# Order of loads at a passage between two stages, one gate tile moved, and filler around 32x32 products in a hybrid encoder block

## The chip, the cores and the metric

The kernel runs on one core of a Trainium2 chip. The metric is the time of one execution in microseconds of device time (us); a kernel is timed in several runs, and their median counts. The engines are named as in the profile: PE (the matrix engine), PEld (its weight loads), DVE (vector), ACT (scalar), POOL (GpSimd) and SP, whose queue issues most of the DMA transfers.

## What is computed

One layer of a bidirectional encoder, 1024 tokens of width 1024, all in 32-bit floats. Cut to what matters here:

```
h   = rms_norm(x)
z   = h @ in_w                      # columns: attention q,k,v | RWKV | two sets of 1024 gates
att = windowed_gqa(q, k, v, sink)   # each token sees +-128 tokens, 8 query heads, 2 key heads
rwk = rwkv7 scans, forward and backward, summed, normed, gated   # 8 heads of 64
x   = x + (tanh-gates * (att @ w_up_attn) + tanh-gates * (rwk @ w_up_rwkv)) @ w_out
x   = x + squared_relu(rms_norm(x) @ w1) @ w2
x   = x + a gated per-layer embedding
```

A gate is written as 1 + tanh(z/2), up to a factor.

## The kernel before

**Products.** A float product on PE is made of three faster ones. Each operand is split into a rounded "hi" part, which ACT casts (`split`, L199), and the rest "lo", which DVE or POOL subtracts (L200). Then hi by hi, lo by hi and hi by lo are summed in one bank. The gates are tiles of 128 columns by 512 tokens: 8 such triples, 24 wide matmuls of 128x512 each (tile `gmm`). Weights of a gate tile come in two transfers (`wst`, halves a and b), which need a free one of the staging buffers; then ACT casts `whi`, the lo engine makes `wlo`, PE multiplies, ACT takes the tanh (`gth`, L333), and SP stores it to DRAM (`g_d`, L334).

**Stages.** First come the norm and the qkv products, then the RWKV operands of four head pairs, which are written to DRAM (`ra_d`, `bk_d`, `v_d`); the 16 gate tiles of the first half of the tokens, gates(0, m), are strewn into it. At its end the keys `kT` and the first queries `qT0`, `qT1` are read back (L756 to L771). Then comes attention in eight blocks n (L908 to L995): its last part at low priority is the rest of the first half's gates and, by `GATT`, the gate tile (1,0), the first of the second half. Into attention two things are mixed for the scans: low products (`lps`), and a triangular inverse by substitution on DVE (31 steps of a product, L837, and a sum, L840, then two transposes `Zn` and `Zt`, L847 and L848, and copies into `zi`, L869).

**The scans.** Sixteen chunks s of 64 tokens, forward and backward at once, in blocks of `NB` = 4. Chunk s multiplies the operands `rac` and `bkc` (`gps`, masked by DVE into `gm`, L1183), transposes (`tmps`, L1200), carries the state (`wy`), applies the inverse (`ups`), updates the state (`sps`) and adds outputs. Between these parts `gap(i)` takes `FILL[i]` steps from a filler, a generator named `beside` (L1000): 15 gate tiles of 24 steps, 6 empty steps (`BRIDGE`), and 16 tiles of 12 steps of the attention's up-projection (`uaps`), 558 steps in all. While a block runs, DVE works on the inverse for the next block, a few steps at a time (`TURNS`). Behind the last chunk of a block stands `end_inverse`: 128 products of 32x32 (`qps<-Zn,lt`), ACT copies them into `Q` (L866), `FILLQ` filler steps run between, then 128 more (`qps<-Zt,Q`), which ACT copies into `zi` (L879, L880). Next comes chunk s+1 with `wy`. A first `end_inverse(0, ...)` stands ahead of the loop, with the products of chunks 0 and 1 around it, and 4 filler steps (`FILL0`) behind each.

**What sets the order.** Products marked `mmo` and DVE steps marked `turn` stay in the program's order; other work is put in by a scheduler by priority and readiness. Each engine runs its list in order, so one instruction that waits holds all behind it; this goes for the DMA issues on the queues of SP and POOL too. The attention result comes back for the up-projection through `load_at` (issues at L1003, tiles named `gm` in the trace, four transfers from `at_d`) and its weights through `load_wu` (`wust`, issues at L1007).

Of the kernel before, what the change touches and what calls it, by code (L numbers as in the profile page):

```python
# [52 lines left out]

FILL0 = 4

GATT = 1
GQ = ((0, 1), (0, 2))

BRIDGE = 6
FILL = (5, 5, 3, 5, 3, 2, 4, 1)  # L60
FILLEND = 2

FILLEP = 11

LEAD = 1
FILLQ = 8
TURNS = ((0, 0, 4), (3, 2, 5), (3, 2, 5), (4, 3, 1))

LOW_AT = (3, 4)
# [77 lines left out]
def block_kernel(ctx: ExitStack, tc: tile.TileContext, I: dict, out: bass.AP):  # L147
# [39 lines left out]
    def after(ins, prev):  # L187

        tc.add_manual_dep(
            ins.ins, prev.ins.name,  # L190
            mybir.DependencyInfo(mybir.DependencyClass.NoSync, mybir.DependencyReason.DATA),
            reason="keep_in_program_order")
# [328 lines left out]
    with ExitStack() as s1:  # L521
# [127 lines left out]
        def fill0(p, i):  # L649

            if p == NP - 1:
                for _ in range(F0[i]):
                    next(gates0)
# [101 lines left out]

        kT = PY.tile([P, 2, 2, T], F32R, name="kT", tag="yk")  # L756
        qT0 = Q0.tile([P, NH, P], F32R, name="qT", tag="q0", bufs=1)
        nc.gpsimd.dma_start(qT0, qT_d[0])
        bands = Q0.tile([P, 3 * P + NH], F32, name="band", tag="q2", bufs=1)
        band = bands[:, 0:3 * P].rearrange("p (b t) -> p b t", b=3)  # L760
        nc.sync.dma_start(band, I["band"])
# [2 lines left out]
        for q in range(4):  # L764
            ts = slice(256 * q, 256 * q + 256)
            a = nc.gpsimd.dma_start(kT[:, :, :, ts], kT_d[:, :, :, ts])
            if q:
                after(a, on_pool[0])
            fill0(NP - 1, 1)
        qT1 = Q0.tile([P, NH, P], F32R, name="qT", tag="q1", bufs=1)  # L770
        nc.gpsimd.dma_start(qT1, qT_d[1])  # L771
        for _ in bonus:
            pass

# [2 lines left out]
    NB = 4  # L777
# [122 lines left out]
    def load_ra(s, d):  # L900
        return nc.sync.dma_start(ra_t[s % NRA, d], ra_d[d, chunk(s, d)])

    def load_bk(s, d):
        return nc.sync.dma_start(bk_t[s % NBK, d], bk_d[d, chunk(s, d)])

    lts, zzs, lows = {}, {}, {}
    with ExitStack() as s2:
# [16 lines left out]
        for n in range(NT):  # L924
            qT = queries(n) if n > 1 else (qT0, qT1)[n]
            k0, k1 = max(n - 1, 0), min(n + 2, NT)
            nk = k1 - k0
            b0 = k0 - (n - 1)
            pTs = []
            for kv in range(2):  # L930
                hs = slice(4 * kv, 4 * kv + 4)
                mx = A3.tile([P, 4], F32, name="mx", bufs=2)
                nm = A3.tile([P, 4], F32, name="nm", bufs=2)
                sums = A3.tile([P, 4], F32, name="sums", bufs=2)
                es = A3.tile([P, 4], F32, name="es", bufs=2)
                sm = A3.tile([P, 4, 3 * P], F32, name="smk", bufs=2)
                for h in range(4):
                    sc = PA.tile([P, nk * P], F32, name="sc", tag="sc", bufs=2)
                    for j in range(2):
                        nc.tensor.matmul(sc, qT[:, 4 * kv + h, :], kT[:, kv, j, k0 * P:k1 * P], start=(j == 0), stop=(j == 1))  # L940
                    nc.vector.tensor_tensor_reduce(
                        out=sm[:, h, 0:nk * P], in0=sc, in1=band[:, b0:b0 + nk, :].rearrange("p b t -> p (b t)"), scale=1.0,
                        scalar=-3.0e38, op0=ALU.add, op1=ALU.max, accum_out=mx[:, h:h + 1])
                nc.vector.scalar_tensor_tensor(out=nm, in0=mx, scalar=-0.125, in1=nsink[:, hs], op0=ALU.mult, op1=ALU.min)
                nc.vector.tensor_tensor(out=es, in0=sink[:, hs], in1=nm, op=ALU.add)
                nc.scalar.activation(out=es, in_=es, func=AF.Exp)
                for h in range(4):
                    nc.scalar.activation(out=sm[:, h, 0:nk * P], in_=sm[:, h, 0:nk * P], func=AF.Exp, scale=0.125, bias=nm[:, h:h + 1],
                                         accum_out=sums[:, h:h + 1])
                nc.vector.tensor_tensor(out=es, in0=es, in1=sums, op=ALU.add)  # L950
                nc.vector.reciprocal(es, es)
                pT = A3.tile([P, 3, 4, P], F32, name="pT", bufs=3)
                pTs.append(pT)
                for h in range(4):
                    if h % 2:
                        nc.scalar.activation(out=sm[:, h, 0:nk * P], in_=sm[:, h, 0:nk * P], func=AF.Copy, scale=es[:, h:h + 1])
                    else:
                        nc.vector.tensor_scalar_mul(sm[:, h, 0:nk * P], sm[:, h, 0:nk * P], es[:, h:h + 1])
                    pt = PA.tile([P, 3, P], F32, name="pt", tag="tp", bufs=3)
                    for j in range(nk):  # L960
                        nc.tensor.transpose(pt[:, j, :], sm[:, h, j * P:(j + 1) * P], ident)
                    if h % 2 == 0:
                        nc.vector.tensor_copy(pT[:, 0:nk, h, :], pt[:, 0:nk, :])
                    else:
                        nc.scalar.copy(pT[:, 0:nk, h, :], pt[:, 0:nk, :])
            po = PA.tile([P, 4, P], F32, name="po", tag="po", bufs=1)
            for j in range(nk):
                for kv in (1, 0):
                    nc.tensor.matmul(po[kv * 64:kv * 64 + 64], V[:, k0 + j, kv * 64:kv * 64 + 64], pTs[kv][:, j, :, :], start=(j == 0), stop=(j == nk - 1))
            at = A3.tile([P, 4, P], F32, name="at", bufs=1)  # L970
            nc.scalar.copy(at, po)
            put = nc.sync.dma_start(at_d[:, :, n * P:(n + 1) * P], at)
            if n == 0:
                low0 = low_products(BI, A2, 2, ps_att, 0, nc.tensor.matmul, put)
                next(low0)
            if n == 1:
                zi = zi_tile(BI, "zi")
            if n in LOW_AT:
                for _ in range(NB // len(LOW_AT)):
                    lts[0] = next(low0)  # L980
            if n == LOW_AT[-1]:
                for d in range(ND):
                    for a in (load_ra(0, d), load_bk(0, d)):
                        after(a, put)
            if n == INV_AT:
                zzs[0] = inverse_turned(BI, inverse(BI, lts[0]))
# [13 lines left out]
    def beside():  # L1000
# [4 lines left out]
        def load_wu(pl, m):  # L1005
            st = pl.tile([P, NP, P], F32, name="wust", tag="wu_st", bufs=2)
            nc.sync.dma_start(st, I["w_up_attn"][m])  # L1007
            return st

        load_at(0)  # L1010
        sts = [load_wu(B, m) for m in range(2)]
        yield from gates(1, range(GATT, 2 * KT), mmo, lo_of=lambda m: nc.vector)
        sW.close()
        sH1.close()
        epi["RWA"] = pool(sR, "rwA", side="right")
# [48 lines left out]
    def fill(n=1 << 30):  # L1064

        for _ in range(n):
            if next(filler, 0) == 0:
                break
# [270 lines left out]
    operand_tiles(B, (2, 3), (1, 2))  # L1339
    for s in (1, 2):  # L1340
        for d in range(ND):
            load_ra(s, d)
            load_bk(s, d)
    load_v(0)
    begin_low(1)
# [5 lines left out]
    was = []  # L1351

    def second_step():
        fill(FILLQ)
        wa = wa_tile()
        for h in range(NH):
            w_own(0, h, wa)
        was.append(w_copy(wa))
        for hf in range(2):
            products(1, hf)  # L1360
            fill(FILL0)
# [5 lines left out]
    for s in range(NCH):  # L1367
        more, nxt = s + 2 < NCH, s + 1 < NCH
        if s % NB == NB - 1 and s // NB < 2:
            begin_low(s // NB + 2)  # L1370

        def gap(i):

            fill(FILL[i] if more else FILLEND)

        def aside(i):

            b = s // NB + 1
            if b < NCH // NB and (s % NB, i) in ((0, 0), (0, 1), (0, 2), (0, 3)):
                low(b, i)  # L1380
            if ep is not None:
                next(ep, None)

        if s == 12:
            epi["E"] = BI
            ep = epilogue(0)
        carried(s)
        w_sum(s, W)
        if more:
            products(s + 2, 0)  # L1390
            load_next(s + 2)
        if nxt:
            load_v(s + 1)
        gap(0)
        aside(0)
        inverse_turn(TURNS[s % NB][0])
        gap(1)
        W = u_part(s, W)
        if more:
            products(s + 2, 1)  # L1400
        inverse_turn(TURNS[s % NB][1])
        gap(2)
        gap(3)
        aside(1)
        if nxt:
            s_part(s)
        y_part(s)
        aside(2)
        gap(4)
        if s % NB == 0 and s // NB < 3:  # L1410
            aside(3)
            inv[0] = inverse_steps(s // NB + 1)
        inverse_turn(TURNS[s % NB][2])
        gap(5)
        if nxt:
            operands(s + 1)
        gap(6)
        gap(7)
        if s % NB == NB - 1 and s // NB < 3:
            end_inverse(s // NB + 1, lambda: fill(FILLQ))  # L1420
        if s % NB or s // NB >= 3:
            aside(3)
    for _ in ep:
# [599 lines left out]
```

## Time and profile before

| what | value |
|---|---|
| three timed runs, us | 1676.85, 1670.13, 1672.34 |
| their median, us | 1672.34 |
| profiled execution, us | 1677.99 |
| its span, first to last instruction, us | 1676.2 |
| mean granted clock of PE | 0.984 |
| attention's end and the passage into the scans | about 455 to 500 us of the span |
| block ends in the scans (second products of 32x32) | 560, 628 and 704 us of the span |

A profile shows one execution. A row of its timeline has the start and the length in us, engine, line, operation, output<-inputs, the shape and the count; in square brackets stands how long the engine was idle before it and what it waited for. The windows give, for a stretch of time, the busy us of each engine and PEclk, the clock that was granted to PE as a share of the full one. "SPq" is the issue of a DMA on SP's queue; the transfer lands later.

### The profile page before, as it was taken

To read this page: it belongs to the slowest core of one execution; us is meant where nothing else is said; L and a number is where in the kernel's file an instruction comes from. 1 tells how busy PE (TensorE), PEld (TensorE's weight loads), DVE (VectorE), ACT (ScalarE), POOL (GpSimd) and SP (SyncE) were. 2 spreads that over 40 slices of the span, in tenths; PEclk is the share of its full clock that TensorE was granted. 3 is DMA by queue.
4 is the path that set the end of the run, shared out by engine and by line. 5 is a ranking of instruction groups with operands and counts; after the bars stand their busy time and mean duration, and the time that the engine had idled before them with its cause. 6 is when DMAs were issued, how large, how long until landed. Compare 5 with 4: busy or idle time off the path is not lost.

```text
span 1676.2 us, 31183 instructions
## 1 busy us (share of the span) xinstructions
PE 1609.2 (96%) x12280; PEld 1302.1 (78%) x12280; DVE 1156.5 (69%) x2103; ACT 820.7 (49%) x1485; POOL 104.8 (6%) x117
## 2 busy tenths in 40 slices
PE   7999999999879999899999999999999999999998
PEld 7987777666558787676778788888888888888887
DVE  6648998476938797876745886667667867675342
ACT  5548887378524443465314454444435445544121
POOL 3430000321200000000000000000000000000000
PEclk9999999999979999899999999999999999999999
DMA  6352555854377464547643154444459865564110
GB/s 224 83 150 88 174 171 182 252 161 145 103 212 199 141 183 129 171 147 231 207 170 113 51 191 146 159 153 143 145 173 351 276 192 172 160 211 145 39 41 38
DMA packets 200579, 269.24 MB, mean 161 GB/s; under 512 B 47728, under 2 KB 103920, under 8 KB 200432
## 3 DMA queue, kind: packets, MB, share of 16 engines
q1 hardware_dynamic: 190176, 253.09, 47.6%
q0 software_dynamic: 10112, 13.63, 3.0%
q8 instruction: 96, 1.57, 0.4%
q10 hardware_dynamic: 144, 0.52, 0.1%
q14 instruction: 51, 0.42, 0.1%
HBM read 186.45 MB, written 80.74 MB: 159 GB/s over the span
## 4 chain that ended last, share of the span: by engine, by line
PE 69%; DVE 14%; DMA 7%; ACT 4%; issue 3%; SPq 1%; POOL 1%; DVEq 0%; POOLq 0%; ACTq 0%
PE ff2ps L1904 18%; PE ff1ps L1652 16%; DMA wst<-in_w_col_dram 3%; PE gmm L225 2%; PE plps L235 2%; PE plps L233 2%; PE plps L231 2%; PE mm L243 2%; PE mm L244 2%; PE mm L245 2%; DVE tmp L1315 1%; DVE Z L1318 1%; DMA g1t<-g_d 1%; PE mmo L245 1%; PE mmo L244 1%
## 5 line engine op out<-in xcount | busy, mean ns | idle before, releaser
L1904 PE MATMUL ff2ps<-th,sl 128*128 128x512 f32 x448 | 174.3, 389 | 0.0
L1904 PE MATMUL ff2ps<-tl,sh 128*128 128x512 f32 x448 | 174.3, 389 | 0.0
L1904 PE MATMUL ff2ps<-th,sh 128*128 128x512 f32 x448 | 173.9, 389 | 0.0
L199 ACT CAST sh<-sst 128x512 fp32r<-128x512 f32 x109 | 67.8, 622 | 107.3 <-PE ff2ps L1904 55.3
L200 DVE TENSOR_TENSOR sl<-sst,sh 128x512 fp32r<-128x512 f32 x109 | 75.0, 688 | 48.3 <-ACT sh L199 48.0
L199 ACT CAST whi<-wst 128x512 fp32r<-128x512 f32 x100 | 60.5, 617 | 88.7 <-DMA wst<-in_w_col_dram 38.5
L1652 PE MATMUL ff1ps<-mh,w1h 128*128 128x512 f32 x256 | 100.3, 392 | 1.8 <-ACT w1h L199 1.8
L1652 PE MATMUL ff1ps<-ml,w1h 128*128 128x512 f32 x256 | 99.9, 390 | 0.0
L1652 PE MATMUL ff1ps<-mh,w1l 128*128 128x512 f32 x256 | 99.6, 390 | 0.0
L1904 PEld LDWEIGHTS ff2ps<-th,sh 128*128 128x128 f32 x448 | 84.0, 188 | 17.9 <-ACT th L199 0.3
L1904 PEld LDWEIGHTS ff2ps<-th,sl 128*128 128x128 f32 x448 | 84.1, 188 | 17.5
L1904 PEld LDWEIGHTS ff2ps<-tl,sh 128*128 128x128 f32 x448 | 84.1, 188 | 17.4
L184 POOL TENSOR_TENSOR rstd<-ms,neghalf 128x1 f32<-128x1 f32 x24 | 14.8, 615 | 1016.3 <-PE ff2ps L1904 572.1
L199 ACT CAST w1h<-w1st 128x512 fp32r<-128x512 f32 x48 | 28.4, 620 | 95.7 <-DMA w1st<-in_w_ff_dram 57.0
L200 DVE TENSOR_TENSOR wlo<-wst,whi 128x512 fp32r<-128x512 f32 x72 | 48.2, 686 | 30.9 <-ACT whi L199 30.8
L200 DVE TENSOR_TENSOR w1l<-w1st,w1h 128x512 fp32r<-128x512 f32 x48 | 31.7, 687 | 50.5 <-ACT w1h L199 50.5
L1652 PEld LDWEIGHTS ff1ps<-mh,w1h 128*128 128x128 f32 x256 | 48.1, 188 | 12.9 <-ACT w1h L199 2.7
L231 PE MATMUL gmm<-hh,whi 128*128 128x512 f32 x136 | 55.1, 405 | 3.0 <-ACT whi L199 2.4
L1652 PEld LDWEIGHTS ff1ps<-mh,w1l 128*128 128x128 f32 x256 | 48.1, 188 | 10.8 <-DVE w1l L200 0.6
L235 PE MATMUL gmm<-hh,wlo 128*128 128x512 f32 x136 | 55.3, 407 | 0.6 <-DVE wlo L200 0.6
L1652 PEld LDWEIGHTS ff1ps<-ml,w1h 128*128 128x128 f32 x256 | 48.1, 188 | 10.0
L233 PE MATMUL gmm<-hl,whi 128*128 128x512 f32 x136 | 54.9, 404 | 0.0
(406 smaller groups left out, 4516.1 us busy)
## 6 DMA issues: line engine op xcount, KB each, us to landing
wst<-in_w_col_dram SPq DMA_DIRECT2D x88, 256.0 KB, 3.6
tst<-in_w_ff_dram SPq DMA_DIRECT2D x80, 256.0 KB, 4.0
w1st<-in_w_ff_dram SPq DMA_DIRECT2D x32, 512.0 KB, 5.1
hid_S<-h SPq DMA_DIRECT2D x64, 256.0 KB, 2.1
sst<-hid_S SPq DMA_DIRECT2D x64, 256.0 KB, 3.0
hid_A<-h SPq DMA_DIRECT2D x48, 256.0 KB, 2.0
sst<-hid_A SPq DMA_DIRECT2D x45, 256.0 KB, 3.8
ra_d<-ra SPq DMA_DIRECT2D x8, 1024.0 KB, 6.1
```

The source lines that it names most:

```text
L199: a = nc.scalar.copy(hi, src)
L200: b = (lo_eng or nc.vector).tensor_tensor(out=lo, in0=src, in1=hi.bitcast(F32), op=ALU.subtract)
L225: tc.keep_in_program_order(nc.tensor.matmul(*a, **kw))
L231: mm(ps, ah, bh, start=(i == 0), stop=False)
L233: mm(ps, ah, bl, start=False, stop=False)
L235: mm(ps, al, bh, start=False, stop=(i == n - 1))
L243: nc.tensor.matmul(ps, ah, bh, start=(i == 0), stop=False)
L244: nc.tensor.matmul(ps, ah, bl, start=False, stop=False)
L245: nc.tensor.matmul(ps, al, bh, start=False, stop=(i == n - 1))
L1315: turn(nc.vector.tensor_tensor(out=tv, in0=Lp[:, t + 1:32, t:t + 1].broadcast_to([P, n, m]), in1=Z[:, t:t + 1, 0:m].broadcast_to([P, n, m] ...
L1652: nc.tensor.matmul(ps, x_[:, k, :], y_[:, k, :], start=start and k + i == 0, stop=k == 3 and i == 2, skip_group_check=True)
L1904: nc.tensor.matmul(banks[bs][i], x_[:, isl], y_, start=fresh and p + j == 0, stop=p == NPR - 1 and j == 2, skip_group_check=True)
```

## The change

It has five parts. (1) `qT0` is asked for behind the first quarter of `kT`, `qT1` behind the last, on POOL's queue. (2) `GATT` is 0, so gate tile (1,0) leaves attention for the head of the filler, where its `wlo` are made by DVE instead of POOL; the weights of tiles (1,0) to (1,4) are asked for on POOL's queue instead of SP's (`GQ`). (3) The loads of the attention result and of the first `wust` come after six gate tiles (`LOADS_AT`), not first. (4) The operand `rac` of chunk 1 is asked for in attention, not at the scans' start. (5) The filler steps are dealt out anew: `FILL` has a row for each chunk of a block, `FILLEND`, `FILLEP` are 3 and 12, `FILLQ` is 9 between the 32x32 products and 7 behind the second set of them.

```diff
-GATT = 1
-GQ = ((0, 1), (0, 2))
+GATT = 0
+GQ = ((0, 1), (0, 2), (1, 0), (1, 1), (1, 2), (1, 3), (1, 4))
+LOADS_AT = 6
-FILL = (5, 5, 3, 5, 3, 2, 4, 1)
-FILLEND = 2
-FILLEP = 11
+FILL = ((4, 4, 2, 4, 2, 2, 3, 1), (5, 5, 3, 5, 3, 2, 4, 1), (5, 5, 3, 5, 3, 2, 4, 1), (5, 5, 3, 5, 3, 2, 3, 0))
+FILLEND = 3
+FILLEP = 12
-FILLQ = 8
+FILLQ = (9, 7)
...
-        nc.gpsimd.dma_start(qT0, qT_d[0])
...
             a = nc.gpsimd.dma_start(kT[:, :, :, ts], kT_d[:, :, :, ts])
             if q:
                 after(a, on_pool[0])
+            else:
+                after(nc.gpsimd.dma_start(qT0, qT_d[0]), a)
...
-        nc.gpsimd.dma_start(qT1, qT_d[1])
+        after(nc.gpsimd.dma_start(qT1, qT_d[1]), a)
...
-                    for a in (load_ra(0, d), load_bk(0, d)):
+                    for a in (load_ra(0, d), load_bk(0, d), load_ra(1, d)):
...
+        yield from gates(1, range(GATT, LOADS_AT), mmo, lo_of=lambda m: nc.vector)
         load_at(0)
         sts = [load_wu(B, m) for m in range(2)]
-        yield from gates(1, range(GATT, 2 * KT), mmo, lo_of=lambda m: nc.vector)
+        yield from gates(1, range(LOADS_AT, 2 * KT), mmo, lo_of=lambda m: nc.vector)
...
-            load_ra(s, d)
+            if s > 1:
+                load_ra(s, d)
             load_bk(s, d)
...
-        fill(FILLQ)
+        fill(FILLQ[0])
...
-            fill(FILL[i] if more else FILLEND)
+            fill(FILL[s % NB if s // NB < 3 else 1][i] if more else FILLEND)
...
-            end_inverse(s // NB + 1, lambda: fill(FILLQ))
+            end_inverse(s // NB + 1, lambda: fill(FILLQ[0]))
+            fill(FILLQ[1])
```

How the lists of the engines change is shown at three places. A number behind a name tells two buffers of one kind apart; the numbers differ between the two programs, and the lines of the changed kernel are one to three higher.

**The passage into the scans.** On SP's queue before, from the last of the first four pairs `la`, `lb` (the inputs of low products) on:

```order
L798 DMA lb<-bk_d 128x4x64
L1003 DMA gm_4612<-at_d 128x512 x2
L1003 DMA gm_4613<-at_d 128x512 x2
L1007 DMA wust<-in_w_up_attn_dram 128x512 x2
L219 DMA wst<-in_w_col_dram 128x512 x2
L901 DMA rac_4615<-ra_d 128x512
L901 DMA rac_4619<-ra_d 128x512
L1192 DMA UV<-v_d 64x512
```

And now, from the same `lb` on:

```order
L800 DMA lb<-bk_d 128x4x64
L903 DMA rac_4579<-ra_d 128x512
L906 DMA bkc_3048<-bk_d 128x512
L903 DMA rac_4583<-ra_d 128x512
L906 DMA bkc_3051<-bk_d 128x512
L1195 DMA UV<-v_d 64x512 x2
L799 DMA la<-ra_d 128x4x64
L335 DMA g_d<-gth 128x512
L800 DMA lb<-bk_d 128x4x64
```

The attention result, `wust` and the two `wst` no longer stand between `lb` and the operands of the next chunks; `wst` is gone to POOL's queue, the attention result and `wust` stand 13 issues behind this `lb`, in front of the loads for a later chunk.

DVE's list at the same place before, from the second transpose of the first inverse on:

```order
L848 STREAM_TRANSPOSE Zt<-Z 128x32x32
L869 COPY zi<-Zn 32x32x32
L869 COPY zi<-Zt 32x32x32 x2
L869 COPY zi<-Zn 32x32x32
L200 TENSOR_TENSOR wlo<-wst,whi 128x512
L1183 TENSOR_TENSOR gm_4612<-gps,gmask 128x384 x2
L200 TENSOR_TENSOR wlo<-wst,whi 128x512
L1183 TENSOR_TENSOR gm_4613<-gps,gmask 128x384 x2
```

And now:

```order
L850 STREAM_TRANSPOSE Zt<-Z 128x32x32
L871 COPY zi<-Zn 32x32x32
L871 COPY zi<-Zt 32x32x32 x2
L871 COPY zi<-Zn 32x32x32
L1186 TENSOR_TENSOR gm_4576<-gps,gmask 128x384 x2
L201 TENSOR_TENSOR wlo<-wst,whi 128x512 x2
L1186 TENSOR_TENSOR gm_4577<-gps,gmask 128x384 x2
L1186 TENSOR_TENSOR gm_4576<-gps,gmask 128x384 x2
```

In both a `wlo` of tile (1,1) stands between the two masks; its weights were the `wst` behind `wust` on SP's queue, and are now the third and fourth `wst` behind attention on POOL's.

**The end of the second 32x32 products, into chunk 4.** PE's list before, at the last two of the products:

```order
L225 MATMUL qps<-Zt,Q 32x32
L225 MATMUL qps<-Q,Zt 32x32
L225 MATMUL wy_6169<-rac_3046,Sc 64x64
L225 MATMUL wy_6170<-rac_3046,Sc 64x64
L225 MATMUL wy_6169<-rac_3046,Sc 64x64
```

And now:

```order
L226 MATMUL qps<-Zt,Q 32x32
L226 MATMUL qps<-Q,Zt 32x32
L226 MATMUL gmm<-hh_90,wlo 128x512
L226 MATMUL gmm<-hh_90,whi 128x512
L226 MATMUL gmm<-hl_91,whi 128x512
L226 MATMUL gmm<-hh_90,wlo 128x512
L226 MATMUL gmm<-hh_90,whi 128x512
L226 MATMUL gmm<-hl_91,whi 128x512
L226 MATMUL gmm<-hh_90,wlo 128x512
L226 MATMUL wy_6132<-rac_3046,Sc 64x64
```

Seven wide matmuls have come between the products and `wy`, here and at chunk 8.

**The third such place, into chunk 12.** ACT's list before, around the copies of the 32x32 products (`rwh` belongs to the RWKV epilogue, `wuhi` and `aTh` are hi parts for the up-projection `uaps`):

```order
L199 CAST rwh_8719<-y 128x512 x4
L866 COPY Q<-qps 32x16x32 x4
L199 CAST wuhi<-wust 128x512
L879 COPY zi<-qps 32x16x32
L880 COPY zi<-qps 32x16x32
L879 COPY zi<-qps 32x16x32
L880 COPY zi<-qps 32x16x32
```

And now:

```order
L868 COPY Q<-qps 32x16x32 x4
L334 ACTIVATE gth<-gmm 128x512
L200 CAST rwh_8676<-y 128x512 x4
L881 COPY zi<-qps 32x16x32
L882 COPY zi<-qps 32x16x32
L200 CAST wuhi<-wust 128x512
L200 CAST aTh<-gm_4576 128x512 x2
L200 CAST aTh<-gm_4577 128x512 x2
L200 CAST wuhi<-wust 128x512
L881 COPY zi<-qps 32x16x32
L882 COPY zi<-qps 32x16x32
```

The filler turns from gates to `uaps` here now, since it has 24 steps more ahead of `uaps`: the first `wuhi` and all of `aTh` come between the two pairs of `zi`. Before, that turn was in chunk 11 (the chunk ahead of this place), and `aTh` was cast there.

## The prediction

> **What bounds the kernel now.** The page's busy row comes first.
>
> ```profile
> PE 1609.2 (96%) x12280; PEld 1302.1 (78%) x12280; DVE 1156.5 (69%) x2103; ACT 820.7 (49%) x1485; POOL 104.8 (6%) x117
> ```
>
> PE is busy 96% of the span, so work on other engines costs only where PE waits for it. A busy PE can still be slow: its clock is granted. So I read PE's list of waits next, and windows of 10 us (columns: length, then busy us of PE, PEld, DVE, ACT, POOL, then the clock, the DMA share and GB/s).
>
> ```profile
> PE tmps L1200 <- DVE gm L1183: 8.9, 2, 8.6
> PE qps L225 <- DVE Zn L1322: 5.1, 1, 5.1
> PE wy L225 <- issue: 4.8, 2, 2.4
> PE gmm L231 <- ACT whi L199: 2.4, 1, 2.4
> PE qps L225 <- ACT Q L866: 1.0, 2, 0.5
> PE uaps L225 <- ACT aTh L199: 0.8, 1, 0.8
> ...
> 310.00:320.00 10.00, 10.00 (x37) 7.83 (x37) 1.36 (x3) 3.41 (x6) 4.00 (x4) 0.83 0.72 204
> 470.00:480.00 10.00, 1.38 (x7) 1.15 (x7) 2.22 (x4) 1.23 (x2) 0.00 (x0) 0.69 0.87 288
> 480.00:490.00 10.00, 10.00 (x210) 7.97 (x209) 1.01 (x2) 4.65 (x8) 0.00 (x0) 0.62 0.84 242
> 560.00:570.00 10.00, 7.63 (x249) 6.22 (x236) 2.94 (x6) 2.41 (x5) 1.10 (x2) 0.66 0.33 108
> 630.00:640.00 10.00, 8.20 (x167) 6.58 (x171) 2.84 (x8) 2.07 (x5) 0.34 (x2) 0.66 0.36 108
> 690.00:700.00 10.00, 4.63 (x112) 3.53 (x114) 9.54 (x22) 3.87 (x7) 0.00 (x0) 0.79 0.70 219
> 700.00:710.00 10.00, 10.00 (x284) 8.21 (x275) 7.74 (x14) 5.23 (x9) 0.00 (x0) 0.53 0.42 133
> ```
>
> The six rows of waits stand at places that the change touches, and behind each longer one the clock is low. A window at 0.66 is 6.8 of 10 us at half clock (1-0.66, doubled); 0.69 and 0.62 together are 13.8 us, 0.79 and 0.53 are 13.6, 0.83 is 3.4. What PE works at half clock takes twice the time, so half of its busy time there is lost.
>
> **The passage.** Next the timeline there, PE first, then the engines behind it.
>
> ```profile
> 454.81 0.39 PE L235 MATMUL gmm<-hh,wlo 128*128 128x512 f32 x1
> ...
> 465.88 0.39 PE L235 MATMUL gmm<-hh,wlo 128*128 128x512 f32 x1
> 466.20 0.90 PE L225 MATMUL gps<-rac,bkc 64*64 64x128 f32 x32
> ...
> 468.15 0.95 PE L225 MATMUL gps<-rac,bkc 64*64 64x128 f32 x32
> ...
> 478.85 1.97 PE L1200 MATMUL tmps<-ident,bkc 128*128 128x128 f32 x8 [8.62 <-DVE gm L1183]
> ...
> 476.99 0.62 ACT L199 CAST whi<-wst 128x512 fp32r<-128x512 f32 x1 [10.03 <-DMA wst<-in_w_col_dram]
> ...
> 464.94 0.69 DVE L869 COPY zi<-Zn 32x1024 f32<-32x1024 f32 x1
> ...
> 477.64 0.69 DVE L200 TENSOR_TENSOR wlo<-wst,whi 128x512 fp32r<-128x512 f32 x1 [9.47 <-ACT whi L199]
> 478.25 1.01 DVE L1183 TENSOR_TENSOR gm<-gps,gmask 128x384 f32<-128x384 f32 x2
> ...
> 468.13 1.99 SPq L1003 DMA_DIRECT2D gm<-at_d  x4
> ...
> 471.17 0.85 SPq L219 DMA_DIRECT2D wst<-in_w_col_dram  x2
> ```
>
> Read backwards: `tmps` needs a bank that the mask `gm` empties; `gm` stands behind a `wlo` on DVE, that waits for ACT's `whi`, that for a `wst` which SP issued at 471.17, behind the attention result and `wust`, which nobody needs yet. That is a queue order, not a lack of work, and the change attacks just this.
>
> What it removes: the wait of 8.62, and the half clock behind it. PE is busy at half clock from 478.85 on, 1.1 us of the first window and 7.6 of the next (1-0.62, doubled): 8.7, so 4.3 go. It also moves 24 wide matmuls out of the tail; 49 of them start within 454.81 to 465.88, so one is (465.88-454.81)/48 = 0.231, and 24 are 5.5. Sum 18.4.
>
> What comes in its place: the tail ends 5.5 earlier, near 460.7. `gps` takes 0.9 and four wide matmuls 0.9, to 462.6. The second `gps` needs the bank of the first, which `gm` empties when DVE has finished the inverse and its copies: 464.94+0.69 = 465.6. That two `wlo` of tile (1,0) no longer run on POOL beside DVE, and run on DVE instead, I let cancel. With half of a `gm` pair, 0.5, this is 466.1: PE waits 3.5. Then `gm` stands behind both `wlo` of tile (1,1), whose weights POOL can ask for when its buffers come free, about where SP issued a `wst` before (457); they land in time by this view's row:
>
> ```profile
> DMA to landing us min/median/max: 2.6/3.1/6.3
> ```
>
> So `tmps` waits 0.5 more, and one wide matmul more stands between (FILLQ 9) at 0.2. The new wait of 3.5 may drop the clock; by the rows above a drop of 6.8 or 3.4 us would cost 3.4 or 1.7, none 0: I take 1.2. Net -(18.4-3.5-0.5-0.2-1.2) = -13.0, between -15 (DVE earlier, no drop) and -10 (the clock low for 13.8 again). What else moves with the tile costs nothing: its casts, `gth` and store go to ACT and SP in stretches where those don't hold PE. POOL's next clearing of `Z` now stands behind the `wst` issues, and DVE needs it only behind the transpose `Lp`; if a late `wst` takes that cover away, the inverse starts later, which is part of the worst end at chunk 4.
>
> **The second products of 32x32 at chunks 4 and 8.**
>
> ```profile
> 555.72 1.29 PE L225 MATMUL qps<-Zn,lt 32*32 32x32 f32 x128
> ...
> 564.29 1.01 PE L225 MATMUL wy<-Sc,rac 64*64 64x64 f32 x25 [2.31 <-issue]
> ...
> 631.80 1.00 PE L225 MATMUL wy<-rac,Sc 64*64 64x64 f32 x25 [2.45 <-issue]
> ...
> q8 instruction: 96, 1.57, 0.4%
> ...
> q8 instruction: 1, 0.02, 1.2%
> ```
>
> `wy` waits for nothing that the profile names. The page's DMA rows hold a queue that fetches instructions, 96 packets of 1.57 MB, so 16 KB each; the window 560 to 565 holds one. PE takes 128 products with 128 weight loads in 1.29 us here, so I read "issue" as PE having outrun its instructions. Seven wide matmuls behind the products take 7x0.231 = 1.6 and need 14 instructions: the fetch goes on beside them, and 2.31 and 2.45 shrink to 0.7 and 0.8. `Q` waits 0.5 at each; nine for eight between takes 0.2 off. The half clock that follows (PE busy from 564.29 for 5.1 us, from 631.80 for 5.9, so 2.6 and 2.9 lost) goes if the short rest no longer drops it. Against it, two wide matmuls fewer ahead of the first products: up to 0.46, I take 0.3. Sum -(1.6+0.2+2.6-0.3) and -(1.6+0.2+2.9-0.3), together -8.5; from -10 to -3, the latter if the clock still drops.
>
> The Trainium skill ("Runtime: NRT & Kernel Launch", "Instruction fetch mechanics") has blocks of 16 KiB, as the packets here, and calls crossing one "mostly hidden"; the 2.31 and 2.45 speak against that at products this small. The Trainium skill ("TensorE: Matmul & The Clock Gate", "The HAM clock gate") lets the clock halve after an idle window of some 3.4 us; here 2.31 was enough by the row 0.66. By that rule the halving would not be these waits' doing and stay, and this term would be -3.
>
> **The third such place, chunk 12.** PE's row, then rows of groups, DVE within 683.5 to 696 and ACT within 690 to 710:
>
> ```profile
> 698.74 1.93 PE L225 MATMUL qps<-Zn,lt 32*32 32x32 f32 x128 [5.10 <-DVE Zn L1322]
> ...
> L200 DVE TENSOR_TENSOR wulo<-wust,wuhi 128x512 fp32r<-128x512 f32 x4 | 2.8, 690 | 1.4 <-ACT wuhi L199 1.4
> L200 DVE TENSOR_TENSOR aTl<-gm,aTh 128x512 fp32r<-128x512 f32 x4 | 2.5, 684 | 0.0
> ...
> L866 ACT COPY Q<-qps 32x512 f32<-32x512 f32 x4 | 2.3, 577 | 2.4 <-PE qps L225 2.3
> L199 ACT CAST rwh<-y 128x512 fp32r<-128x512 f32 x4 | 2.2, 614 | 2.2 <-DVE y L1283 2.2
> L199 ACT CAST wuhi<-wust 128x512 fp32r<-128x512 f32 x2 | 1.2, 618 | 4.1 <-DMA wust<-in_w_up_attn_dram 4.1
> L879 ACT COPY zi<-qps 32x512 f32<-32x512 f32 x2 | 1.2, 577 | 2.5 <-PE qps L225 2.5
> ```
>
> DVE's start of the up-projection, 2.8+2.5 and an idle 1.4, stood ahead of `Zn`; it now comes later, so `Zn` is over 5 us earlier and the wait of 5.1 shrinks to 0.5. With it go `aTh`'s 0.8, and a half clock of 13.6 us of which PE is busy from 698.74 on: 1.3 us up to 700, then 9.4 (1-0.53, doubled), half of which is 5.3. Removed 10.7. But PE meets `uaps` right behind the second products, and ACT has first `Q` 2.3, `gth` 0.6 (a tile of the size of `wuhi`), `rwh` 2.2, two `zi` 1.2, `wuhi` and one `aTh` at 0.6: 7.5 from the first products' end, where PE is done after some 3.8 (the wait for `Q`, then 1.3 of products). A wait of 3.7 takes the old one's place, and the last `zi` adds about 0.9. Between the waits of 2.3 (2.6 lost to the clock) and 5.1 (5.3 lost), 3.7 loses 4. Net -(10.7-0.5-3.7-0.9-4) = -1.6, from -8 (clock untouched) to +3 (`aTl` and `zi` later).
>
> **Where the filler goes.** 24 steps more are in the scans' filler. Ahead of the loop 1 more is used (counted); a block of four chunks takes 4x28+8 = 120 before and 22+28+28+26+16 = 120 now; chunks 14 and 15 take 16 more, the last epilogue 7 more.
>
> ```profile
> 709.00:791.00 82.00, 76.10 (x996) 57.28 (x990) 57.82 (x106) 47.84 (x77) 0.00 (x0) 1.00 0.56 181
> ```
>
> 23x0.231 = 5.3; PE idles 5.9 in this whole stretch, in small gaps. I let 1.8 of it hide: +3.5, from +1 to +5.3.
>
> **kT and queries.** `qT0` and `qT1` leave the place ahead of `wst` on POOL's queue; the wait of 2.4 for `whi` and its 3.4 us of half clock (1.7) may go, or `qT0` may meet the next weights: -1, from -3.5 to +1.5.
>
> **Sum.** -13.0-8.5-1.6+3.5-1 = -20.6. The profiled execution took 1677.99, 5.65 above the median of the runs shown (1672.34): it becomes 1657.4, and the median, by the same distance, 1651.7. All best ends give -35.5, all worst -3.2; both at once are unlikely, and 1639 to 1665 takes in most of it.
>
> One window more, for the third rival, of the first block:
>
> ```profile
> 500.00:550.00 50.00, 49.71 (x1115) 40.27 (x1114) 42.25 (x108) 21.04 (x44) 0.00 (x0) 0.99 0.66 180
> ```
>
> **Rivals.** (a) The clock decides, not the waits: 3.5 and 3.7 drop it for 13.8 each, and the rests of 0.7 and 0.8 still drop it. For it: 2.31 sufficed for 6.8 us. Loses 3.1 at the passage, 1.3 at chunk 12, 5.5 at chunks 4 and 8: gain 10.7, time 1662. (b) "issue" is no fetch that wide matmuls cover, or the fetch starts only behind them: 3.2 of stalls and 5.5 of clock stay, gain 11.9, time 1660; against it, one packet in that very window. (c) DVE becomes the bound in a block: at 690 to 700 it is busy 9.54 of 10, though in the first block it has room, by the row above (42.25 of 50). Then the 8.5 of two blocks shrink to 4: time 1656.  (d) It ends slower: on SP's queue `wust` now waits for POOL's `wst` of tile (1,3), and operands of later chunks queue behind it. Tile (1,3)'s buffer comes free when (1,0) is done, about 476 (24 steps along PE's list), and `wust` goes out about 480; before, loads for the next chunks went out between 480 and 487, with PE 14 us further back, so that some 14 us are in hand. From 495 on each us of delay is a us of PE's; to eat up 20.6 and 8.4 more, the landing must be near 524, over 40 us behind its issue. The slowest `wst` at the passage took 6.3. Then 1681 or more. (e) The lists move but the waits stay, as other transfers fill the rings (DMA share 0.87 at 470 to 480): time 1672.
>
> **Chances.** Forecast 0.60, (a) 0.13, (b) 0.12, (c) 0.08, (d) 0.03, (e) 0.04. Half a per cent, 8.4 us, is about what a measurement of this kernel can tell from no change: faster means below 1664. The forecast is so in nearly all its spread (0.58), (a) and (b) in four fifths (0.20), (c) wholly: 0.86; slower is (d), 0.03; the rest, 0.11, is the same.
>
> **What would show it.** Right: `tmps` no longer waits for `gm` over 2 us, a wait of about 3 at the second `gps` in its place, "issue" below 1 ahead of `wy`, no window at 0.66 behind chunks 4 and 8, `uaps` waiting 3 to 4 for `aTh` behind chunk 12's products, PE fuller in the last chunks. Wrong: `whi` still waiting for `wst` at the passage, "issue" unchanged behind the seven matmuls, or PE waiting for `rac`, `bkc`, `la` or `UV` near 490 to 510.

## The result, and the profile after

Over 14 runs each, the changed kernel takes 1665.67 us (median, 1662.07 to 1670.42) and the kernel before 1674.85 (1670.13 to 1679.79). The ratio is 0.9948, with a 95% interval of 0.9936 to 0.9960: 8.7 us less, between 6.7 and 10.7. The direction was as forecast, the size was under half of it, and the median lies 0.7 above the range.

The profiled executions differ by more, 1677.99 to 1664.77, so 13.2. The one of before lay 3.1 above its median, the one of the change 0.9 below: of the 13.2 that the traces show, 4 are the choice of the executions.

First PE's waits after the change, over the whole span (columns: us in total, times, the longest):

```profile
PE ups L226 <- DVE W L1241: 4.9, 3, 2.0
PE uaps L226 <- ACT aTh L200: 3.6, 1, 3.6
PE gps L226 <- DVE gm L1186: 2.5, 1, 2.5
PE gmm L232 <- ACT whi L200: 2.4, 1, 2.4
PE qps L226 <- ACT Q L868: 1.8, 3, 0.9
PE qps L226 <- DVE Zn L1325: 1.7, 2, 1.5
...
PE gps L226 <- issue: 1.6, 1, 1.6
PE wa L226 <- issue: 1.6, 1, 1.6
...
PE wy L226 <- issue: 0.2, 1, 0.2
```

The waits that the change aimed at are gone: `tmps` for `gm` (8.6), `qps` for `Zn` (5.1, now 1.7), "issue" ahead of `wy` (4.8, now 0.2). A list of new ones stands in their place: `W`, `aTh`, the second `gps`, two of "issue" at the passage. How much was won in all is seen in windows whose ends are the same work in both: from attention's last product to the first product of the output projection, and its parts. The kernel before:

```profile
454.09:522.49 68.40, 58.49 (x1075) 45.50 (x1075) 35.87 (x74) 23.91 (x47) 3.65 (x4) 0.88 0.76 209
522.49:659.53 137.04, 130.38 (x3121) 106.37 (x3121) 111.02 (x260) 57.60 (x118) 2.21 (x4) 0.95 0.54 158
659.53:735.53 76.00, 67.57 (x1443) 54.22 (x1442) 61.95 (x136) 35.18 (x60) 0.00 (x0) 0.91 0.50 157
735.53:842.14 106.61, 98.91 (x745) 74.14 (x745) 81.33 (x134) 50.58 (x81) 0.00 (x0) 1.00 0.65 208
454.09:842.14 388.05, 355.35 (x6381) 280.23 (x6381) 290.16 (x599) 167.27 (x303) 5.86 (x8) 0.94 0.60 181
```

And the changed one, to the same points (the state updates `sps` of chunks 1, 9 and 13 divide them):

```profile
453.03:512.75 59.72, 50.70 (x1046) 39.10 (x1045) 33.27 (x70) 21.54 (x43) 5.46 (x10) 0.94 0.85 230
512.75:643.33 130.58, 125.54 (x3122) 102.63 (x3121) 110.37 (x260) 56.95 (x117) 2.23 (x4) 1.00 0.56 164
643.33:716.42 73.09, 65.70 (x1449) 52.86 (x1448) 60.82 (x133) 36.34 (x63) 0.00 (x0) 0.95 0.49 154
716.42:828.54 112.12, 104.20 (x769) 79.26 (x768) 83.81 (x138) 51.97 (x82) 0.00 (x0) 0.98 0.66 211
453.03:828.54 375.51, 346.14 (x6382) 273.85 (x6381) 288.26 (x597) 166.80 (x303) 7.68 (x14) 0.98 0.62 187
```

The last row of each is the reading that matters. PE does the same 6381 matmuls. It is idle for 388.05-355.35 = 32.7 us before and 375.51-346.14 = 29.4 after: only 3.3 of the waits have gone. It is busy for 9.2 us less with the same work, because the clock is 0.98 instead of 0.94. So of 12.5 us three quarters are half clock that no longer happens, and the waits have mostly moved. These two executions are not alone in it: the mean clock of the change's 14 runs is 0.990 to 0.996, with a median of 0.993; that of 25 other runs of the kernel before, taken beside e1 to e4, is 0.984 to 0.991, with a median of 0.988.

### The profile page after: what moved, and what is told of

Read it like the earlier page. It is cut to its first block, busy times and chain, and to the rows that moved or that the text cites. A ratio compares the mean times of both kernels' runs of the same rounds, so it can differ in the third digit from the quotient of the medians.

```text
span 1663.0 us, 31182 instructions
## 1 busy us (share of the span) xinstructions
PE 1599.4 (96%) x12280; PEld 1294.3 (78%) x12280; DVE 1156.7 (70%) x2105; ACT 820.2 (49%) x1485; POOL 107.5 (6%) x125
## 3 DMA queue, kind: packets, MB, share of 16 engines
q8 instruction: 96, 1.57, 0.4%
## 4 chain that ended last, share of the span: by engine, by line
PE 75%; DVE 12%; DMA 6%; ACT 4%; issue 3%; POOL 1%; SPq 0%; DVEq 0%; ACTq 0%; POOLq 0%
PE ff2ps L1909 18%; PE ff1ps L1657 16%; PE gmm L226 4%; DMA wst<-in_w_col_dram 2%; PE uaps L226 2%; PE mm L244 2%; PE mm L245 2%; PE mm L246 2%; PE plps L236 2%; PE plps L234 2%; PE plps L232 2%; DMA g1t<-g_d 1%; PE wy L226 1%; PE gps L226 1%; PE mmo L246 1%
## 5 line engine op out<-in xcount | busy, mean ns | idle before, releaser
L201 DVE TENSOR_TENSOR w1l<-ssum,w1h 128x512 fp32r<-128x512 f32 x64 | 42.9, 687 | 15.2 <-ACT w1h L200 15.2
```

Of the source, the lines that this page charges most:

```text
L201: b = (lo_eng or nc.vector).tensor_tensor(out=lo, in0=src, in1=hi.bitcast(F32), op=ALU.subtract)
```

## The experiments

Two theories stood for what the trace raised first, the waits for `W`: T, that six filler steps taken out of chunks 0, 4 and 8 bring PE to `ups` before DVE is done; and R, that the new loads and POOL's queue make DVE late. A third, P, came up on the way. All ratios are against runs of the kernel before on the same chip; an interval stands behind each.

**e1, the loads alone.**

```diff
-FILL = ((4, 4, 2, 4, 2, 2, 3, 1), ..., (5, 5, 3, 5, 3, 2, 3, 0))
-FILLEND = 3
-FILLEP = 12
-FILLQ = (9, 7)
+FILL = ((5, 5, 3, 5, 3, 2, 4, 1),) * 4
+FILLEND = 2
+FILLEP = 11
+FILLQ = (8, 0)
```

> The changed kernel with the filler numbers of before (28 steps in every chunk, 8 between the 32x32 products, none behind, 2 and 11 at the end); loads and the moved gate tile stay changed. Theory T (PE waits for DVE's W in chunks 1, 5 and 9 because six filler steps were taken out of chunks 0, 4 and 8): no wait for W over 0.4 us there, 'issue' of 2.3 to 2.5 us ahead of wy at chunks 4 and 8 as before, and a time 6 to 9 us below before (passage 11, seven to eight given back late). Rival R (the waits for W come from the new loads: DVE's and POOL's work ahead of the inverse is late): a wait for W of 1 us or more in chunk 1, and 4 to 7 us below before.

Measured: 0.9982 (0.9969 to 0.9995), 3 us below before, a miss of T's time, though its waits are right: none for `W` over 0.4 in those chunks. PE's waits and two windows behind chunks 4 and 8:

```profile
PE wy L226 <- issue: 5.6, 2, 2.9
PE uaps L226 <- ACT aTh L200: 4.1, 1, 4.1
...
550.00:570.00 20.00, 16.47 (x501) 13.11 (x501) 9.48 (x20) 8.74 (x19) 1.11 (x2) 0.91 0.40 107
610.00:630.00 20.00, 16.25 (x474) 13.40 (x477) 11.83 (x18) 7.98 (x15) 1.11 (x2) 0.83 0.38 121
```

The passage is as short as in the change (60.8 us for the same stretch, 59.7 there, with five matmuls more in it), but "issue" grew to 2.9 with the half clock behind it, and the filler's turn to `uaps` now waits 4.1 for `aTh`. R falls: the new loads alone make no wait for `W`.

**e2, the filler alone**: the new `FILL`, `FILLEND`, `FILLEP` and `FILLQ` in the kernel before.

> The kernel before with the new filler numbers alone (rows 22, 28, 28, 26; 9 between and 7 behind the products; 3 and 12 at the end). Theory T: 'issue' ahead of wy at chunks 4 and 8 below 0.3 us and no half clock behind it, but waits for W of 1 to 2 us in chunks 1, 5 and 9: 2 to 5 us below before. Rival R: no waits for W, so 7 to 9 us below before.

Measured: 0.9995 (0.9980 to 1.0011), no difference.

```profile
PE tmps L1200 <- DVE gm L1183: 10.6, 1, 10.6
PE gps L225 <- DVE ysq L1141: 4.0, 1, 4.0
PE ups L225 <- DVE W L1238: 3.5, 3, 1.9
...
PE wy L225 <- issue: 1.0, 1, 1.0
```

The seven matmuls bring "issue" from 4.8 to 1.0 and the waits for `W` come (3.5), as T said. But the passage's wait, on a transfer, grew by the 2 us that PE came sooner, and for the last epilogue 61 steps were left instead of 78, taken 12 at a time, so that its `gps` waits 4.0. Loads and filler alone give 3 and 0.8 us, together 8.7: each exposes a wait that the other covers.

**e3, 28 steps in chunks 0, 4, 8**, with 26, 26 and 24 in the others.

```diff
-FILL = ((4, 4, 2, 4, 2, 2, 3, 1), (5, 5, 3, 5, 3, 2, 4, 1), (5, 5, 3, 5, 3, 2, 4, 1), (5, 5, 3, 5, 3, 2, 3, 0))
+FILL = ((5, 5, 3, 5, 3, 2, 4, 1), (5, 5, 3, 5, 3, 2, 3, 0), (5, 5, 3, 5, 3, 2, 3, 0), (4, 4, 3, 5, 3, 2, 3, 0))
```

> The changed kernel with 28 filler steps in chunks 0, 4 and 8 instead of 22, the six taken from the other three chunks of the block (26, 26, 24), so that a block uses as many as in the change. Theory T: the waits for W (1.8, 1.8 and 2.0 us in chunks 1, 5, 9) fall below 0.4 each, and the time is 3 to 6 us below the changed kernel, 1660 to 1663. Rival R: the waits stay and the time is within 1 us of the changed kernel.

Measured: 0.9938 (0.9916 to 0.9960), not to be told from the change's 0.9948, so T's time is a miss. (The three waits for `W` in the change are 1.78, 1.16 and 1.95: the one in chunk 5 is 1.2 and not 1.8, here and in e9.)

```profile
PE qps L226 <- DVE Zn L1325: 4.3, 3, 1.5
...
PE ups L226 <- DVE W L1241: 1.6, 3, 0.9
```

`W` fell from 4.9 to 1.6 and `Zn` rose from 1.7 to 4.3. PE waits for DVE's inverse nearly as long as in the change (5.9 for both, 6.6 there), only at the block's other end.

**e4, nothing behind the second products**: rows of 28, 28, 28 and 27 and `FILLQ = (9, 0)`.

> The changed kernel with nothing behind the second 32x32 products, and the seven steps given back to the gaps (28, 28, 28, 27). If the seven wide matmuls cover an instruction fetch: 'issue' of about 2.3 us ahead of wy at chunks 4 and 8 and a half clock behind it come back, 7 to 8 us in all, waits for W are gone (5 us), and the time is 1 to 3 us above the changed kernel. If 'issue' has another cause that went with the loads: it stays below 0.3, and the time is 5 us below the changed kernel.

Measured: 0.9971 (0.9954 to 0.9987), 4 us above the change. The waits for `W` are gone and "issue" is back:

```profile
PE wy L226 <- issue: 2.9, 2, 1.5
...
545.00:565.00 20.00, 18.35 (x545) 14.60 (x544) 12.89 (x29) 11.09 (x25) 1.11 (x2) 1.00 0.51 144
610.00:630.00 20.00, 18.25 (x547) 14.60 (x546) 12.88 (x31) 10.27 (x22) 1.10 (x2) 1.00 0.52 146
```

The second expectation falls: "issue" goes with the seven matmuls, not with the loads. The profiled execution (1663.63) is the fastest of ten: here the rests of 1.5 did not drop the clock. In the nine others the mean clock was 0.987 to 0.991 against 0.992, and the time 1666.7 to 1675.0. What the seven matmuls are worth is thus partly clock, and shows in the median, not in this trace.

**e5 and e10, the gate tile back in attention** (`GATT = 1`, POOL's queue with the weights of (1,0) and (1,1)); e10 also has `FILLEND = 2` and `FILLEP = 11`.

> The changed kernel with gate tile (1,0) back in attention; on POOL's queue only the weights of (1,0) and (1,1), so that DVE has two wlo and not four ahead of the mask. Theory L (moving the tile loses: its 24 wide matmuls cost 5.5 us in the tail, but the wait of 2.5 at the second gps and 5.3 us late are there only since it left): the wait at the second gps falls below 0.5 us, the stretch from chunk 14 to the first matmul of the RWKV projection gives back under 1 us instead of 5, and the time is 3 to 8 us below the changed kernel. Rival M (the tile's leaving is what shortens the passage): the first 32x32 products come 5 us later than in the changed kernel and the time is 0 to 4 us above it.

> The gate tile back in attention as in e5, and the numbers for the last chunks and the last epilogue as before the change (2 and 11), since 24 steps fewer are left for them. If e5 lost at the end because its filler ran out (waits of 3.8 and 4.0 us there, both with a half clock): these waits fall below 1 us each, and the time is 3 to 6 us below e5 and 2 to 6 below the changed kernel. If they have another cause: they stay, and the time is that of e5.

Measured: e5 0.9956 (0.9940 to 0.9972), e10 0.9950 (0.9930 to 0.9970). Both equal the change. In e5:

```profile
PE gps L226 <- DVE ysq L1144: 4.0, 1, 4.0
PE mups L226 <- ACT rwh L200: 3.8, 1, 3.8
```

Theory M falls, since the passage is short with the tile in attention too: the first 32x32 products come 1.7 us later than in the change, not 5. L falls in its time. The two waits at the end were filler that ran out, as e10 says: with its numbers none there is over 1.6 (below 1 was expected), and the last stretch takes 108.0 us instead of 112.1. Its time is a miss even so; against the 4.1 stand the 5.5 us of the tile's matmuls, which are in the tail again. Where the tile stands is worth nothing that these runs can tell.

**e6, the second set of products twice.**

```diff
         for i in range(32):
             k = i % 2
-            mm(qss[0][g[2 * k], i // 2, :], ...)
-            mm(qss[1][g[3 - 2 * k], i // 2, :], ...)
+            for _ in range(2):
+                mm(qss[0][g[2 * k], i // 2, :], ...)
+                mm(qss[1][g[3 - 2 * k], i // 2, :], ...)
```

> The changed kernel with each product of the second 32x32 set issued twice in a row (the second time over the first, with the same result), at all four places: 128 products and 128 weight loads more at each, 256 instructions, the content of one fetch packet. If PE outruns its instructions there (two packets in one such place before lay 3.8 us apart): 3 to 4 us more at each place, 'issue' rows of 1.5 us and more at all four, and 9 to 16 us more in all. If 'issue' is no fetch: 1.3 us more at each place, 5 us in all, and no new 'issue'.

Measured: 1.0044 (1.0027 to 1.0060), that is 16 us above the change by the two ratios (0.0096 of 1675), and 17.5 between the two profiled executions.

```profile
PE qps L226 <- issue: 11.4, 4, 5.1
...
488.47 0.21 PE L226 MATMUL qps<-Zt,Q 32*32 32x32 f32 x1 [5.14 <-issue]
...
560.57 0.25 PE L226 MATMUL qps<-Zt,Q 32*32 32x32 f32 x1 [2.76 <-issue]
```

The doubled products themselves cost 1.3 us a place. PE now rests among them, with nothing to wait for but its next instruction: 11.4 in four places, and the half clock behind. "Issue" is instructions used up faster than they come. The packets of the queue that fetches instructions (q8) say the same: the rest that ends at 488.47 ends 1.4 us behind a packet that takes 485.86 to 487.08. In all 14 profiled executions 36 rests called "issue" of 0.6 us and more lie between 450 and 850 us, and each ends 1.2 to 1.7 us behind the end of such a packet. With some 51 packets in these 400 us, that would happen by chance to one rest in fifteen.

**e7, seven steps more behind the second products at the passage.**

```diff
-    fill(FILL0)
+    fill(FILL0 + FILLQ[1])
```

> The changed kernel with seven more filler steps behind the second 32x32 products at the passage, where only four stood. Theory F (the fetch stall of 1.6 us at the gps behind them and its 3.4 us of half clock are what the passage lost against the forecast): both vanish, first lps 2 to 3 us earlier against the wide matmuls' own 1.6, time 1 to 4 us below the changed kernel. Rival D (DVE's start of the next inverse decides chunk 1): both vanish, but the wait for W in chunk 1 stays at 1.8 or grows, and the time is within 1 us.

Measured: 0.9945 (0.9928 to 0.9962), the same as the change; D has the time, neither has the waits. "Issue" at `gps` stayed (2.0 instead of 1.6), so F falls; but the waits for `W` are gone in chunks 1, 5 and 9, against D, although chunks 4 and 8 have their 22 steps. So T falls too: it isn't the number of steps. Why F falls is seen in the trace:

```profile
486.72 0.35 PE L226 MATMUL gps<-rac,bkc 64*64 64x64 f32 x9 [2.00 <-issue]
```

The eleven wide matmuls behind the products take 481.20 to 483.98, and the packet that this rest waits for starts only then, at 483.97, and ends at 485.14. Ahead of chunk 4 in the change a packet takes 550.54 to 552.09, beside the seven (550.27 to 552.1). The filler at the passage stood ahead of the fetch and not beside it.

A gate tile has 24 steps and a block 120, five tiles: each block starts at the same place within a tile, and seven steps ahead of the loop shift where tiles end in all three. That is theory P, and DVE's rows of chunk 0 in the changed kernel show what a tile's end does:

```profile
499.12 0.69 DVE L201 TENSOR_TENSOR wlo<-wst,whi 128x512 fp32r<-128x512 f32 x1 [0.20 <-PE gmm L226]
499.73 1.26 DVE L1303 COPY Lc<-lt 32x256 f32<-32x256 f32 x4
501.02 0.69 DVE L201 TENSOR_TENSOR wlo<-wst,whi 128x512 fp32r<-128x512 f32 x1
501.63 2.27 DVE L1303 COPY Lc<-lt 32x256 f32<-32x256 f32 x4
503.93 2.06 DVE L1310 STREAM_TRANSPOSE Lp<-Lc 128x1024 f32<-128x1024 f32 x1
...
508.17 0.74 DVE L1241 TENSOR_TENSOR W<-W,wy 128x256 f32<-128x256 f32 x2
...
502.78 0.97 POOL L1312 MEMSET Z<- 128x1024 f32 x1
...
508.64 0.27 PE L226 MATMUL ups<-W,zi 64*64 64x64 f32 x2 [1.78 <-DVE W L1241]
```

Two `wlo` have got among the last copies `Lc`, ahead of the transpose `Lp` (in chunk 8 one stands right between the copies and `Lp`). In chunk 0 POOL's clearing of `Z`, late behind its `wst`, also runs beside the copies, four of which take 2.27 instead of 1.2; in e9 twelve take 4.34 beside it in chunk 0, and 3.56 in chunk 8, where it isn't beside them. `Lp`, four steps of the inverse and then `W` are later by that, and PE waits.

**e9, the same 22 steps dealt earlier** in chunks 0, 4 and 8.

```diff
-FILL = ((4, 4, 2, 4, 2, 2, 3, 1), ...
+FILL = ((5, 5, 3, 5, 1, 1, 1, 1), ...
```

> The changed kernel with the same 22 filler steps in chunks 0, 4 and 8, but dealt earlier in the chunk (5, 5, 3, 5, 1, 1, 1, 1): a gate tile then ends in the fourth gap and not the fifth. Theory P (the waits for W come from the place, not the number, of the steps: the tile's end sets off a wlo pair, which in the changed kernel falls on DVE between the last copies Lc and the transpose Lp): no wait for W over 0.5 us in chunks 1, 5, 9, with 22 steps. Theory T (fewer steps): the waits of 1.8, 1.8, 2.0 stay. In both, by what the other runs showed, a part turns up as a wait of the 32x32 products for Zn; time 0 to 4 us below the changed kernel under P, the same under T.

Measured: 0.9925 (0.9906 to 0.9945), 4 us below the change with intervals that overlap.

```profile
PE qps L226 <- DVE Zn L1325: 1.9, 3, 1.5
PE ups L226 <- DVE W L1241: 1.8, 3, 1.2
```

With 22 steps the waits for `W` are gone in chunks 1 and 5 (0.4 and 0.3 are left); in chunk 9 1.16 of 1.95 stays. `Zn` did not take their place (1.9 against 1.7). P holds in two places of three; the third stays open.

**e8, the gate weights back on SP's queue** (`GQ = ((0, 1), (0, 2))`); **e11**, this and e9 together; **e12**, these and the tile of e10.

> The changed kernel with the gate weights of the second half of the tokens back on SP's queue; the attention result and wust still come after six gate tiles. If the order of the loads on SP's queue did it: the passage is as short as in the changed kernel within 1 us (no wait of tmps for gm over 1 us), and the time within 1.5 us. If POOL's queue was needed (SP's transfers ahead of wst hold it): a wait of tmps or of a wide matmul for whi of 2 us or more near 465 to 490, and 3 us or more above the changed kernel.

> The gate weights on SP's queue as in e8 and the earlier filler of e9 together. If both are gains of their own: 1 to 4 us below e8. If the block is bound by DVE's chain, so that a wait for W only turns into one for Zn: the same as e8 within 1.5 us.

> All that looked good together: weights on SP's queue, the gate tile back in attention with 2 and 11 at the end, the earlier filler in chunks 0, 4, 8. If the tile's move was a loss: 2 to 5 us below e11. If it was none: within 1.5 us of e11 or above.

Measured: e8 0.9918 (0.9900 to 0.9936), e11 0.9942 (0.9923 to 0.9961), e12 0.9923 (0.9907 to 0.9940). In e8 and e11 `tmps` doesn't wait for `gm`: with the gate tile moved, the order of the loads did it, and POOL's queue wasn't needed for that. In e11, and then in e12:

```profile
PE gmm L226 <- ACT gth L334: 5.5, 1, 5.5
...
PE tmps L1203 <- DVE gm L1186: 3.7, 1, 3.7
```

With the tile in attention (e12), SP asks for a `wst` at 465.77, behind `la` and `lb`; `whi` waits 5.1 for it, and `tmps` waits for `gm` again. In e5 and e10, with the tile in attention and POOL's queue, it doesn't. And SP's queue with the weights on it is late with the stores `g_d`: ACT's `gth` waits for them and a wide matmul behind it, 5.5 us in e11 near 496 and 2.0 in e8, by the times (`gth` ends at 495.58, the matmul starts at 495.63). So POOL's queue does spare PE waits, though the times don't show it. e8 comes out 5 us below the change, more than expected, its interval just touching the change's; e11 adds e9's edit and loses again. No version stands clearly below the change.

## Why the prediction was wrong

**The base.** The forecast set the profiled execution against three runs. Their median was 1672.34, that of 14 is 1674.85: 2.5 us of the 14 by which the time was missed. The rest is the size, 20.6 against 9.2. Of these 11.4, 7.4 are seen in the traces (13.2 where 20.6 was forecast), and 4 are the choice of the executions: the forecast priced the half clock of one that lay above its median.

**The passage.** Forecast -13.0; the windows give 59.72-68.40 = -8.7. The reading was right: `tmps` waits for no `gm`, and the second `gps` takes its place with 2.5 (3.5 forecast). The step that failed is the list of "what comes in its place", which put the instruction fetch at nothing. I had read "issue" as fetch at chunks 4 and 8, and did not ask where else many small products stand close together once 8.6 us of waiting and a half clock no longer give the fetch time. PE's rows there:

```profile
464.26 1.97 PE L226 MATMUL gps<-rac,bkc 64*64 64x128 f32 x32 [2.52 <-DVE gm L1186]
475.76 0.68 PE L226 MATMUL wa<-UV,gm 64*64 64x64 f32 x17 [1.57 <-issue]
...
487.47 0.27 PE L226 MATMUL gps<-rac,bkc 64*64 64x64 f32 x2 [1.60 <-issue]
...
460.00:470.00 10.00, 7.45 (x84) 5.57 (x76) 6.79 (x11) 2.81 (x5) 1.08 (x2) 0.83 1.14 307
490.00:500.00 10.00, 10.00 (x268) 7.93 (x268) 4.68 (x13) 5.87 (x14) 0.00 (x0) 0.89 0.58 152
```

Two stalls of 1.6, each of which ends 1.4 to 1.6 us behind a packet of q8 (473.11 to 474.15 and 484.85 to 486.08), a half clock behind the second of them (488.7 to 492.1; 0.89 at 490 to 500), and 1.78 for `W` in chunk 1: PE is idle 9.0 us in this stretch against 9.9 before. The wait of 2.5 at the second `gps` dropped the clock for 3.4 us too (0.83 at 460 to 470). The two half clocks lose about 3.4 together, where 1.2 was taken.

The windows also don't hold the same filler. The new `FILL` takes six steps out of chunk 0, and they come back in the stretch of chunk 12 (29 matmuls fewer here, six more there). At 0.231 each that is 1.4 us: in the forecast's terms the passage won 7.3, and chunk 12 won 4.3.

**Chunks 4 and 8.** Forecast -8.5; -6.5 by the windows (137.04 to 130.58). "Issue" fell further than forecast, 0.2 instead of 1.5, and no window is below full clock:

```profile
550.00:570.00 20.00, 19.81 (x558) 16.00 (x545) 12.32 (x29) 10.47 (x24) 1.11 (x2) 1.00 0.60 158
610.00:630.00 20.00, 19.63 (x656) 15.71 (x658) 12.22 (x26) 11.43 (x24) 1.12 (x2) 1.00 0.42 125
```

The half clocks behind didn't stay, so that the term is far from -3. (The prediction's "2.31 was enough" misreads the row, since the clock before fell 0.6 us into that rest; the last section has it.) What the term lacks went to the waits for `W` (1.2 and 2.0 in chunks 5 and 9, the latter at this stretch's end), which are rival (c) in a form that it did not have: not DVE's whole load, but a `wlo` at the wrong place of its list.

**Chunk 12.** Forecast -1.6, measured 73.09-76.00 = -2.9. `uaps` waits 3.6 for `aTh`, 3.7 forecast. The half clock was sized too large:

```profile
680.00:700.00 20.00, 15.35 (x409) 12.08 (x408) 14.17 (x25) 13.78 (x25) 0.00 (x0) 0.83 0.66 211
```

It is 6.8 us, from 683.3 to 690.1, and PE works in it only from 686.02 on: 2 us lost where 4 was forecast. The forecast's sum has a slip besides: 5.1, 0.8 and 5.3 are 11.2, and 10.7 has the remaining wait of 0.5 taken off already, which is then taken off again; the term should read -2.1.

**The filler's end.** Forecast +3.5, measured 112.12-106.61 = +5.5. PE is busy for 5.3 more (104.20-98.91) with 24 more matmuls and a little half clock, and idle 7.9 us against 7.7: nothing of it hid. I take it that the idle places belong to chains in which PE is a link, so that work which doesn't fill the very gap only lengthens the chain; no run shows this by itself.

**kT and queries.** Forecast -1; attention's end is 1.1 earlier, and that is chance. Attention's first product is at 329.2 before and at 326.0 in the change, but at 326.5 in e2 too, where nothing ahead of it is changed; attention ends at 452.0 in e2, and anywhere from 450.7 to 453.7 in the other runs. The wait of 2.4 for `whi` is still there.

**The sum.** -1.1-8.7-6.5-2.9+5.5 and +0.4 in the rest is the 13.2 of the traces, up to rounding. Of the rivals, (a) came in small: the waits of 2.5 and 3.6 are followed by half clock, but for 3.4 and 6.8 us and not 13.8, and in all the clock rose. (b), (d) and (e) did not come: the seven matmuls cover the fetch at chunks 4 and 8, PE waited for nothing behind `wust`, and the old wait is gone.

**What stays open.** What makes a packet of q8 start when it does, and so where filler would have to stand at the passage to be beside the fetch; the transfers of the attention result and `wust` go out there at that time, but no run took them away. Why a wait for `W` stays in chunk 9 in e9. Whether e8 is better than the change by itself.

## What to carry to other kernels

Add up PE's idle time and its slowed work over a stretch with the same ends in both kernels before pricing a list of waits one by one: waits that lie on one chain replace each other, and only the sum tells what was won. When a long wait goes, list what it had been paying for on the quiet, here instructions that came in while PE stood still. Filler hides a fetch only where it runs beside it, so look in the trace for when the packet starts. And where work is dealt out by counts, ask where its ends fall, not only how many steps there are: the steps of a tile set off work on other engines.

## What the runs showed of the hardware

PE can use up instructions faster than they come: 128 products of 32x32 with their weight loads take 1.29 us, and where 256 more instructions stood (e6), PE rested 2.4 to 5.1 us at three of four places. Such a rest ends 1.2 to 1.7 us behind a packet of q8, in 36 cases of 36.

Whether the clock falls depends on more than the length of a rest. In the change a rest of 1.57 (to 475.76) leaves it whole, and one of 1.60 (to 487.47) is followed by half clock from 488.7 on. Rests of 1.4 and 1.5 (e4) did not drop it in the profiled execution, while the mean clock of the other runs of that kernel was lower (0.987 to 0.991 against 0.992). At chunk 4 before the change it fell at 562.6, when PE had stood still for 0.6 us:

```profile
562.00:563.00 1.00, 0.00 (x0) 0.00 (x0) 0.00 (x0) 0.99 (x2) 0.49 (x2) 0.80 0.86 295
```

In the change's execution, up to 800 us, it falls at 307.8, 447.7, 464.8, 488.7, 683.3 and 754.9 us. The distances are 41, 5, 7, 57 and 21 times 3.413 us, and a half clock lasts once or twice that. The Trainium skill ("TensorE: Matmul & The Clock Gate", "The HAM clock gate") speaks of a free-running window, by which a run's chance would decide; these distances and the spread of the runs agree.
